# The weights' lower parts made by VectorE alone, in a two-layer decoder trunk on one core

## The chip, the cores and the metric

The kernel runs on one core of a Trainium2 chip, as one program. The metric is the device time of one execution in microseconds, the median of the runs shown. Before the change it is 2773.92 us (three runs: 2771.38, 2773.92 and 2775.31).

## The reference, cut to what matters

Two layers, each of four sub-layers, in float32 on 512 tokens of width 1024. Every sub-layer stands between two RMS norms, and its output is added to the residual `x`:

```
for l in range(2):
    h = rmsnorm(x, ff1_pre_g[l])
    x = x + 0.5 * rmsnorm(swiglu(h, ff1_w1[l], ff1_w3[l], ff1_w2[l]), ff1_post_g[l])
    h = rmsnorm(x, mix_pre_g[l])
    x = x + rmsnorm(token_mixer(h, ...), mix_post_g[l])        # pooling, sparse attention, gated MLP
    h = rmsnorm(x, mem_pre_g[l])
    x = x + rmsnorm(memory_cross_attention(h, ...), mem_post_g[l])
    h = rmsnorm(x, ff2_pre_g[l])
    x = x + 0.5 * rmsnorm(swiglu(h, ff2_w1[l], ff2_w3[l], ff2_w2[l]), ff2_post_g[l])
```

Nearly all the arithmetic is products of the 512 tokens with weight matrices that are read once each; the queue that brings them moves 255.56 MB.

## The kernel before, in words

**Products in parts.** A float32 operand is cut into an upper part (rounded to the matmul type fp32r) and a lower part (what the rounding left). A product is then three matmuls: upper by upper, upper by lower, lower by upper (`mm3`). So each weight block of 128x1024 numbers passes through four hands: a DMA from SP's queue brings it into one of three buffers `raw`; ScalarE copies it, rounded, into the upper half of one of four buffers `wh` (L394); then one subtraction, raw minus upper, fills the lower half; then TensorE uses both. The subtraction is the instruction that the change is about. `Weights.parts` issues it through `Builder.lo`, which adds up two estimates, one for VectorE (a start when its modelled queue is free, 0.07 us and 1.05 ns per column) and one for GpSimd (0.1 us and 2.4 ns per column). GpSimd gets it if its estimated end is earlier than VectorE's plus `self.spare`.

**`spare`** is the allowance, in us, that the program sets by stage: -0.5 at first; 4.0 from the last loop of `token_out` to the middle of the next `first_blocks`; 2.5 in the mixer, from the second compression to the end of `spatial`. With two idle queues and 1024 columns GpSimd's estimate is 2.56 us and VectorE's 1.15 us, so it is GpSimd at 4.0 and at 2.5, and VectorE at -0.5.

**Order.** The order of all engines' instructions is written out by the host before the run. `Clock` is a model of the engines: tasks are generators in a heap, each resumed at its modelled time, and what a task issues stands in its engine's queue in that order. Each engine runs its queue in order. Every modelled end therefore moves what comes after it in all the queues, TensorE's among them. The model has one free time per engine, and no case in which two engines hold each other up.

**Boundaries.** Each sub-layer ends in `token_out`: four tiles of 128 tokens (m = 0 to 3), each with two banks of 512 columns, and the last four weight blocks of the second half are used tile by tile, so that the tiles end one after another. A tile that is done goes through `chain`: sum of squares (ScalarE), product with the gain (VectorE, `f<-ps,f`), the sum `sty<-ssy`, one small step, the power on GpSimd (`sty<-v,neghalf`, L468), the update of the residual in two halves on VectorE (`x<-f,sty,x`, L402, both inputs in SBUF), squares of the new `x` on ScalarE, a second power on GpSimd (`st`), the pre-norm of the next sub-layer on VectorE (`f<-x,st,f`, L402), eight transposes on TensorE (L437), and the split into `hh` (ScalarE) and `hlo` (VectorE). `first_blocks` starts the next sub-layer: four weight blocks by the first 256 tokens as soon as tiles 0 and 1 are split, then the same four blocks by the last 256 tokens when tiles 2 and 3 are. There are seven such boundaries between the eight sub-layers. The four `wh` buffers are held by the last four blocks of `token_out` until its last tile, so the four blocks of `first_blocks` are made in the boundary itself.

Of the kernel before, what the change touches and what calls it, by code (L numbers as in the profile page):

```python
# [10 lines left out]
F32 = mybir.dt.float32  # L11
# [3 lines left out]
OP = mybir.AluOpType  # L15
# [152 lines left out]
class Slots:  # L168


    def __init__(self, tiles):
        self.free = [(0.0, i, t) for i, t in enumerate(tiles)]
        self.n = len(self.free)
        self.gone = ()
# [133 lines left out]
class Weights:  # L308
# [39 lines left out]
    def parts(self, k):  # L348
        b, n = self.b, k.cols
        raw, hi, lo = k.raw[:, :n], k.hl[:, 0, :n], k.hl[:, 1, :n]  # L350
        yield b.act(hi, raw, AF.Copy)
        r = b.lo(lo, raw, hi)
        self.raws.put(r, k.raw)
        k.raw = None
        k.ready = r
        self.pump()
# [21 lines left out]
def size(ap):  # L378
    n = 1
    for s in ap.shape[1:]:  # L380
        n *= s
    return n


class Builder:
    def __init__(self, tc, d, out):
        self.tc, self.nc, self.d, self.out = tc, tc.nc, d, out
        self.ck = Clock()
        self.spare = -0.5

# [19 lines left out]
    def gtt(self, out, a, b, op):  # L412
        self.nc.gpsimd.tensor_tensor(out, a, b, op)  # L413
        return self.ck.op("g", 0.1 + 0.0024 * size(out))

    def lo(self, out, src, hi):

        ck = self.ck
        n = size(out)
        v = max(ck.free["v"], ck.now) + 0.07 + 0.00105 * n  # L420
        g = max(ck.free["g"], ck.now) + 0.1 + 0.0024 * n
        if g < v + self.spare:
            return self.gtt(out, src, hi.bitcast(F32), OP.subtract)
        return self.tt(out, src, hi.bitcast(F32), OP.subtract)

    def mm(self, out, w, x, first, last):
        ck = self.ck
# [19 lines left out]
    def split(self, hi, lo, src, scale=None, bias=None):  # L447

        if scale is not None:
            yield self.act(hi, src, AF.Copy, scale=scale)  # L450
            return self.stt(lo, src, scale, hi.bitcast(F32), OP.mult, OP.subtract)
        if bias is not None:
            yield self.act(hi, src, AF.Identity, bias=bias)
            return self.stt(lo, src, bias, hi.bitcast(F32), OP.add, OP.subtract)
        yield self.act(hi, src, AF.Copy)
        return self.tt(lo, src, hi.bitcast(F32), OP.subtract)
# [134 lines left out]
    def first_blocks(self, keys):  # L591

        ck = self.ck
        got = []
        for m in (0, 1):
            ck.reach(("T", self.at, m))
        for key in keys:
            blk, bank = self.ws.next(key), ck.get(self.ps)
            self.proj(blk, bank, 0, 256)
            got.append((blk, bank))  # L600
        for m in (2, 3):
            ck.reach(("T", self.at, m))
        self.spare = -0.5
        for blk, bank in got:
            self.proj(blk, bank, 256, 512)
            self.ws.release(blk)
            yield bank

    def token_out(self, l, ph, name, lhs, ready, nk, scale, tail):

        nc, ck, ws = self.nc, self.ck, self.ws
        a, b = scale
        pg = self.load_gain(l, ph, "post")
        after = self.after
        norm = self.pre_norms(self.at + 1, self.load_gain(*after, "pre")) if after else None
        ws.ahead = 4
        nb = nk // 2
        tail = min(tail, nb)
        t0 = {}
        left = [2 * NT]  # L620

        def products(blk, i, m, bank):
            for kk in range(2):
                k = 2 * i + kk
                c = slice(kk * 512, (kk + 1) * 512)
                lh, ll = lhs(k, m)
                self.mm(bank, lh, blk.hl[:, 0, c], k == 0, False)
                self.mm(bank, lh, blk.hl[:, 1, c], False, False)
                self.mm(bank, ll, blk.hl[:, 0, c], False, k == nk - 1)

        def squares(m, h, bank):
            t = yield from ck.take(self.f)
            r = self.act(self.junk, bank, AF.Square, accum_out=self.ssy[:, m, h:h + 1])
            q = self.tt(t[:, :512], bank, pg[h][:, :512], OP.mult)
            left[0] -= 1
            if not left[0]:
                self.f.put(q, *pg)
            self.ps.put(max(r, q), bank)
            return t, r, q

        def half(m, bank):
            t, r, q = yield from squares(m, 0, bank)
            t0[m] = (t, max(r, q))

        def chain(m, bank):
            t1, r, q = yield from squares(m, 1, bank)
            yield r
            st = self.small.tile([128, 2], F32, name="sty", bufs=6)
            yield self.tt(st[:, 0:1], self.ssy[:, m, 0:1], self.ssy[:, m, 1:2], OP.add)
            yield (yield from self.rstd(st[:, 1:2], st[:, 0:1], a, b))  # L650
            xs = [self.x[:, m, h * 512:(h + 1) * 512] for h in range(2)]
            rs = []
            for h, t in enumerate((t0[m][0], t1)):
                r = self.stt(xs[h], t[:, :512], st[:, 1:2], xs[h], OP.mult, OP.add)
                self.f.put(r, t)
                rs.append(r)
            for h in range(2):
                yield rs[h]
                if after:
                    r = self.act(self.junk, xs[h], AF.Square, accum_out=self.ssx[:, m, h:h + 1])  # L660
                else:
                    nc.sync.dma_start(self.out[m * 128:(m + 1) * 128, h * 512:(h + 1) * 512], xs[h])
            if after:
                yield r
                yield from norm(m)

        banks = [ck.get(self.ps) for _ in range(NT)]
        for i in range(nb):
            for kk in range(2):
                ck.reach(ready(2 * i + kk))  # L670
            blk = ws.next((l,) + name + (0, i))
            for m in range(NT):
                products(blk, i, m, banks[m])
            ws.release(blk)
        for m in range(NT):
            ck.spawn(half(m, banks[m]), ck.now + ck.LAT)
        banks = [ck.get(self.ps) for _ in range(NT)]
        for i in range(nb - tail):
            blk = ws.next((l,) + name + (1, i))
            for m in range(NT):  # L680
                products(blk, i, m, banks[m])
            ws.release(blk)
        blks = []
        self.spare = 4.0
        for m in range(NT):
            for i in range(tail):
                if m == 1:
                    ws.ahead = 2
                if m == 0:
                    blks.append(ws.next((l,) + name + (1, nb - tail + i)))  # L690
                blk = blks[i]
                products(blk, nb - tail + i, m, banks[m])
                if m == NT - 1:
                    ws.release(blk)
            ck.spawn(chain(m, banks[m]), ck.now + ck.LAT + (2.0 if m == 2 and after else 0.0))
# [44 lines left out]
    def mixer(self, l, ph):  # L740
        tc, nc, d, ck = self.tc, self.nc, self.d, self.ck
        F, H, PS, ws, at = self.f, self.hl, self.ps, self.ws, self.at
        with tc.tile_pool(name=f"mix{l}", bufs=1) as pool, \
# [152 lines left out]
            def compress(s, i):  # L896
                if i == 0:
                    ck.reach(("B", at, s))
                    hid[s] = (ck.get(PS), ck.get(PS))
                blk = ws.next((l, "cw1", s, i))  # L900
                for a in range(4):
                    lp = 4 * i + a
                    mv = B[s][lp // 8][:, (lp % 8) * 64:(lp % 8) * 64 + 64]
                    for hh in range(2):
                        self.mm(hid[s][hh][:, :64], blk.raw[:, a * 256 + hh * 128:a * 256 + hh * 128 + 128], mv,
                                lp == 0, lp == 15)
                ws.release(blk)
# [95 lines left out]
                        self.mm(o, self.hlo[:, k, t], blk.hl[:, 0, c], False, k == KD - 1)  # L1003
                ws.release(blk)

            self.spare = 2.5
            compress(1, 0)
            vb = [ck.get(PS) for _ in range(NT)]
            for i in range(4):
# [121 lines left out]
            def spatial():  # L1131
                ck.reach(("wst", at))
                for m in range(NT):
                    ck.reach(("vg", at, m))
                for g in range(4):
                    bank = ck.get(PS)
                    for m in range(NT):
                        self.mm(bank[:, m * 128:(m + 1) * 128], VG[m][:, g * 128:(g + 1) * 128],
                                wst[:, g * 128:(g + 1) * 128], True, True)
                    ck.spawn(gate_units(g, bank), ck.now + ck.LAT)  # L1140
                F.put(ck.now, *VG, wst, rows["lng"], rows["lnb"], rows["gm"])
                self.spare = -0.5

            tasks = self.attention(few, dict(KS=KS, KW=KW, V=V, VC=VC, Q=Q, gates=gates, msel=msel, mwin=mwin,
                                                 mcmp=mcmp, zero=zero, rows=rows))
# [432 lines left out]
```

## Time and profile before

| | us |
|---|---|
| median of the runs shown | 2773.92 |
| the profiled execution | 2770.11 |
| its span, first to last instruction | 2768.1 |
| TensorE busy in matmuls | 2716.3 |
| VectorE busy | 1420.6 |
| ScalarE busy | 1037.9 |
| GpSimd busy | 323.8 |

The profiled execution lies 3.8 us under the median of the runs and 2.0 us over its span. Its mean granted TensorE clock is 0.997 of full speed. In the 40 slices of the span TensorE is at nine tenths or more in 38. The chain that ended last is 88% TensorE and 9% VectorE.

Names in the rows: PE is TensorE, PEld its weight load, DVE is VectorE, ACT ScalarE, POOL GpSimd, SP the DMA queue. L429 is a matmul, L437 a transpose, L394 any ScalarE activation, L398 any `tensor_tensor` and L402 any `scalar_tensor_tensor` of VectorE, L413 any `tensor_tensor` of GpSimd: one line serves many places, so the tiles' names tell which one it is. `wh<-raw,wh` is always the subtraction that makes a lower part.

### The profile page before, as it was taken

What the parts mean: (1) busy time and instruction counts of PE and PEld (TensorE: products, weight loads), DVE (VectorE), ACT (ScalarE), POOL (GpSimd) and SP (SyncE); (2) the same over time, 40 slices, a digit from 0 to 9 for tenths busy, and PEclk for the clock granted to TensorE, in tenths of its full rate; (3) what the DMA queues carried; (4) which work ended last, traced back from release to release, by engine and by line L of the source; (5) the groups of instructions that cost most, each with busy time, mean ns of one, the idle gap of its engine ahead of it and who ended that gap; (6) DMA issues with size and microseconds to landing.
All of it is one profiled execution on the core that took longest, in us unless ns stands there. A gap on an engine that the chain in (4) does not pass through costs nothing.

```text
span 2768.1 us, 34462 instructions
## 1 busy us (share of the span) xinstructions
PE 2716.3 (98%) x13624; PEld 2298.3 (83%) x13624; DVE 1420.6 (51%) x2536; ACT 1037.9 (37%) x1894; POOL 323.8 (12%) x299
## 2 busy tenths in 40 slices
PE   7999999999999999999999999999999999999998
PEld 7888888887888888888888888888778898888887
DVE  4443254889536564432354432639885465544422
ACT  3222234456435443222232222435564354432222
POOL 0000021411222020000010000213112220200000
PEclk9999999999999999999999999999999999999999
DMA  3232223311233322322223322242122343223222
GB/s 145 96 114 96 99 92 123 101 58 62 84 114 122 115 77 99 114 99 98 78 99 106 108 93 98 89 135 88 54 69 80 111 138 107 73 103 107 99 92 76
DMA packets 77971, 270.45 MB, mean 98 GB/s; under 512 B 10161, under 2 KB 10673, under 8 KB 77809
## 3 DMA queue, kind: packets, MB, share of 16 engines
q1 hardware_dynamic: 71568, 255.56, 27.3%
q0 software_dynamic: 3136, 10.25, 1.5%
q10 hardware_dynamic: 3104, 2.45, 0.3%
q8 instruction: 106, 1.74, 0.3%
q14 instruction: 57, 0.46, 0.1%
HBM read 266.12 MB, written 2.10 MB: 97 GB/s over the span
## 4 chain that ended last, share of the span: by engine, by line
PE 88%; DVE 9%; ACT 1%; issue 1%; POOL 1%; DMA 0%; ACTq 0%; SPq 0%; DVEq 0%; POOLq 0%
PE ps L429 85%; PE ps L437 2%; DVE x L402 2%; DVE hl L398 1%; ACT junk L394 1%; DVE wh L398 1%; DVE f L402 1%; DVE f L407 1%; DVE f L398 1%; DVE ast L398 1%; DVE f L1227 1%; DVE mf L407 0%; DVE mf L1227 0%; DVE sty L398 0%; DMA raw<-in_ff_w_dram 0%
## 5 line engine op out<-in xcount | busy, mean ns | idle before, releaser
L429 PE MATMUL ps<-hh,wh 128*128 128x512 f32 (+1 forms) x4864 | 1399.1, 369 | 1.9 <-ACT hh L394 1.4
L429 PEld LDWEIGHTS ps<-hh,wh 128*128 128x128 f32 x4864 | 883.9, 189 | 149.9 <-ACT hh L394 1.8
L429 PE MATMUL ps<-hlo,wh 128*128 128x512 f32 (+1 forms) x2432 | 897.3, 369 | 0.1
L398 DVE TENSOR_TENSOR wh<-raw,wh 128x1024 fp32r<-128x1024 f32 x402 | 505.6, 1260 | 601.8 <-ACT wh L394 601.2
L394 ACT ACTIVATE wh<-raw 128x1024 fp32r<-128x1024 f32 x462 | 485.2, 1052 | 726.3 <-PE ps L429 430.5
L429 PEld LDWEIGHTS ps<-hlo,wh 128*128 128x128 f32 x2432 | 460.8, 189 | 72.4 <-DVE v L409 0.4
L429 PE MATMUL ps<-wh,hl 128*128 128x512 f32 x2016 | 468.9, 390 | 0.0
L429 PEld LDWEIGHTS ps<-wh,hl 128*128 128x128 f32 x2016 | 376.8, 188 | 77.2
L413 POOL TENSOR_TENSOR wh<-raw,wh 128x1024 fp32r<-128x1024 f32 (+2 forms) x60 | 146.7, 2449 | 1281.9 <-ACT wh L394 1281.9
L398 DVE TENSOR_TENSOR f<-ps,f 128x512 f32<-128x512 f32 (+1 forms) x169 | 116.6, 690 | 313.9 <-PE ps L429 209.5
L429 PE MATMUL ps<-wh,g 128*128 128x512 f32 x960 | 222.2, 390 | 0.0
L429 PEld LDWEIGHTS ps<-wh,g 128*128 128x128 f32 x960 | 179.3, 188 | 36.7
L429 PE MATMUL ps<-hl,wh 128*128 128x512 f32 (+1 forms) x960 | 194.9, 350 | 0.0
L429 PEld LDWEIGHTS ps<-hl,wh 128*128 128x128 f32 x960 | 152.3, 190 | 20.5
L394 ACT ACTIVATE hl<-f 128x512 fp32r<-128x512 f32 (+1 forms) x75 | 47.3, 630 | 252.6 <-DVE f L398 213.0
L437 PE MATMUL ps<-ident,f 128*128 128x128 f32 (+1 forms) x573 | 100.7, 285 | 33.2 <-DVE f L402 30.9
L394 ACT ACTIVATE hl<-ps 128x512 fp32r<-128x512 f32 (+2 forms) x180 | 80.4, 468 | 102.4 <-PE ps L429 81.7
L398 DVE TENSOR_TENSOR hl<-ps,hl 128x512 fp32r<-128x512 f32 (+2 forms) x180 | 91.8, 528 | 43.5 <-ACT hl L394 42.1
L437 PEld LDWEIGHTS ps<-ident,f 128*128 128x128 f32 (+1 forms) x573 | 70.4, 143 | 48.6 <-DVE f L402 36.3
L402 DVE SCALAR_TENSOR_TENSOR f<-f,ps 128x512 f32<-128x512 f32 x120 | 81.7, 681 | 46.4 <-PE ps L429 42.0
L394 ACT ACTIVATE g<-f 128x512 fp32r<-128x512 f32 x40 | 25.3, 632 | 181.2 <-DVE f L398 181.2
L402 DVE SCALAR_TENSOR_TENSOR x<-f,sty,x 128x512 f32<-128x512 f32 x64 | 78.5, 1267 | 10.2 <-POOL sty L468 10.2
(186 smaller groups left out, 1991.7 us busy)
## 6 DMA issues: line engine op xcount, KB each, us to landing
raw<-in_ff_w_dram SPq DMA_DIRECT2D x264, 512.0 KB, 3.5
raw<-in_wf_dram SPq DMA_DIRECT2D x80, 512.0 KB, 3.5
raw<-in_cw_dram SPq DMA_DIRECT2D x16, 512.0 KB, 3.6
raw<-in_wmo_dram SPq DMA_DIRECT2D x16, 512.0 KB, 3.5
raw<-in_wq_dram SPq DMA_DIRECT2D x16, 512.0 KB, 3.6
raw<-in_wk_dram SPq DMA_DIRECT2D x16, 512.0 KB, 3.8
raw<-in_wv_dram SPq DMA_DIRECT2D x16, 512.0 KB, 3.8
raw<-in_wo_dram SPq DMA_DIRECT2D x16, 512.0 KB, 3.6
```

The costliest lines, as they stand in the source:

```text
L394: self.nc.scalar.activation(out, src, func, accum_out=accum_out, **kw)
L398: self.nc.vector.tensor_tensor(out, a, b, op)
L402: self.nc.vector.scalar_tensor_tensor(out, a, s, b, op0, op1)
L407: self.nc.vector.tensor_scalar(out, a, s0, None, op0=op0)
L413: self.nc.gpsimd.tensor_tensor(out, a, b, op)
L429: self.nc.tensor.matmul(out, w, x, start=first, stop=last)
L437: self.nc.tensor.transpose(out, src, self.ident)
L1227: nc.vector.tensor_tensor_reduce(p[:, po:po + w], bank[:, ps:ps + w], mask, -0.125, 3.0e38, OP.add, OP.min, st[:, br, 0:1])
```

## The change

The choice is taken out: `Builder.lo` and the five places that set `spare` go, and `Weights.parts` always issues the subtraction on VectorE, with the same operands. The estimate that the planner books for it is VectorE's.

```diff
@@ class Weights, parts
         yield b.act(hi, raw, AF.Copy)
-        r = b.lo(lo, raw, hi)
+        r = b.tt(lo, raw, hi.bitcast(F32), OP.subtract)
         self.raws.put(r, k.raw)
@@ class Builder
-        self.spare = -0.5
...
-    def lo(self, out, src, hi):
-
-        ck = self.ck
-        n = size(out)
-        v = max(ck.free["v"], ck.now) + 0.07 + 0.00105 * n
-        g = max(ck.free["g"], ck.now) + 0.1 + 0.0024 * n
-        if g < v + self.spare:
-            return self.gtt(out, src, hi.bitcast(F32), OP.subtract)
-        return self.tt(out, src, hi.bitcast(F32), OP.subtract)
@@ first_blocks
-        self.spare = -0.5
@@ token_out
-        self.spare = 4.0
@@ mixer
-            self.spare = 2.5
...
-                self.spare = -0.5
```

GpSimd keeps its other work: the powers of the norms, the element-wise products and sums of the mixer (`gtt` elsewhere), copies of zeros, and the DMAs of gains and biases.

## Rows read from the trace of the kernel before

**Rows 1.** The page, busy us (share of the span) xinstructions by engine.
```profile
PE 2716.3 (98%) x13624; PEld 2298.3 (83%) x13624; DVE 1420.6 (51%) x2536; ACT 1037.9 (37%) x1894; POOL 323.8 (12%) x299
```
**Rows 2.** Waits of TensorE over the span: total us, times, longest us.
```profile
PE ps L437 <- DVE f L402: 30.9, 18, 8.0
```
**Rows 3.** GpSimd's subtractions: xcount: ns min/median/max, first and last start us, forms.
```profile
L413 POOL TENSOR_TENSOR wh<-raw,wh x60: 1401/2405/3187, 362.5 to 2740.3; 128x1024 fp32r<-128x1024 f32 x54, 128x840 fp32r<-128x840 f32 x4, 128x560 fp32r<-128x560 f32 x2
```
**Rows 4.** Windows over the seven boundaries (28 us each): their sum and mean.
```profile
sum 196.00, PE 178.65 PEld 164.10 DVE 156.10 ACT 96.30 POOL 99.08; mean PE 25.52 PEld 23.44 DVE 22.30 ACT 13.76 POOL 14.15
```
**Rows 5.** Timeline of GpSimd in one boundary: start us, us, instruction.
```profile
1384.59 2.41 POOL L413 TENSOR_TENSOR wh<-raw,wh 128x1024 fp32r<-128x1024 f32 x1 [1.59 <-ACT wh L394]
...
1387.87 5.21 POOL L413 TENSOR_TENSOR wh<-raw,wh 128x1024 fp32r<-128x1024 f32 x2
...
1395.67 2.51 POOL L413 TENSOR_TENSOR wh<-raw,wh 128x1024 fp32r<-128x1024 f32 x1
```
**Rows 6.** Timeline of VectorE in the same boundary.
```profile
1385.73 1.29 DVE L398 TENSOR_TENSOR sty<-ssy 128x1 f32<-128x1 f32 x1
...
1388.32 5.31 DVE L402 SCALAR_TENSOR_TENSOR x<-f,sty,x 128x512 f32<-128x512 f32 x2
...
1395.21 3.52 DVE L402 SCALAR_TENSOR_TENSOR x<-f,sty,x 128x512 f32<-128x512 f32 x2 [0.39 <-POOL sty L468]
1398.65 1.40 DVE L402 SCALAR_TENSOR_TENSOR f<-x,st,f 128x512 f32<-128x512 f32 x2
...
1406.14 0.69 DVE L398 TENSOR_TENSOR hlo<-ps,hh 128x512 fp32r<-128x512 f32 x1 [0.70 <-ACT hh L394]
```
**Rows 7.** Timeline of TensorE there: first block, late transposes, second halves.
```profile
1388.28 0.28 PE L429 MATMUL ps<-hh,wh 128*128 128x256 f32 x1
...
1399.45 1.12 PE L437 MATMUL ps<-ident,f 128*128 128x128 f32 x4 [2.74 <-DVE f L402]
...
1404.88 0.60 PE L437 MATMUL ps<-ident,f 128*128 128x128 f32 x4
1405.23 0.48 PE L429 MATMUL ps<-hh,wh 128*128 128x256 f32 x2
```
**Rows 8.** Windows there: PE, PEld, DVE, ACT, POOL busy (x), PEclk, DMA share, GB/s.
```profile
1388.00:1396.00 8.00, 8.00 (x67) 7.92 (x67) 7.54 (x10) 4.03 (x8) 6.45 (x5) 1.00 0.55 196
1400.00:1403.00 3.00, 3.00 (x18) 3.00 (x17) 2.05 (x6) 1.20 (x2) 0.55 (x1) 0.62 0.24 94
```
**Rows 9.** Window there of VectorE alone: DVE busy (x), PEclk, DMA share, GB/s.
```profile
1383.00:1407.00 24.00, 20.07 (x26) 0.93 0.25 88
```
**Rows 10.** VectorE by tile over the span: xcount: ns min/median/max, first and last start.
```profile
L402 DVE SCALAR_TENSOR_TENSOR x<-f,sty,x x64: 739/750/2889, 369.2 to 2764.0; 128x512 f32<-128x512 f32 x64
L398 DVE TENSOR_TENSOR sty<-ssy x32: 142/149/1760, 368.1 to 2762.3; 128x1 f32<-128x1 f32 x32
...
L398 DVE TENSOR_TENSOR wh<-raw,wh x402: 1204/1225/2674, 14.0 to 2734.8; 128x1024 fp32r<-128x1024 f32 x134
```
**Rows 11.** VectorE by shape over the span: xcount | busy us, mean ns | idle before.
```profile
L402 DVE SCALAR_TENSOR_TENSOR x<-f,sty,x 128x512 f32<-128x512 f32 x64 | 78.5, 1267 | 10.2 <-POOL sty L468 10.2
...
L398 DVE TENSOR_TENSOR sty<-ssy 128x1 f32<-128x1 f32 x32 | 15.9, 498 | 0.0
```
**Rows 12.** GpSimd's powers by tile: xcount: ns min/median/max, first and last start.
```profile
L468 POOL TENSOR_TENSOR sty<-v,neghalf x32: 547/548/560, 368.6 to 2762.8; 128x1 f32<-128x1 f32 x32
L468 POOL TENSOR_TENSOR brs<-v,neghalf x8: 544/656/997, 505.0 to 1884.2; 128x1 f32<-128x1 f32 x8
```
**Rows 13.** Windows of the mixers' stretch with 2.5, both layers (columns as rows 8).
```profile
462.00:524.00 62.00, 61.14 (x350) 53.40 (x349) 33.95 (x55) 22.18 (x47) 29.15 (x15) 1.00 0.41 133
1836.00:1898.00 62.00, 60.01 (x349) 52.53 (x349) 37.32 (x56) 22.44 (x48) 28.60 (x15) 1.00 0.40 125
```
**Rows 14.** VectorE in the first of these: one shape by groups, as rows 11.
```profile
L398 DVE TENSOR_TENSOR V<-f,V 128x256 fp32r<-128x256 f32 x3 | 3.5, 1153 | 0.0
```
**Rows 15.** Timeline of VectorE there: one of these three.
```profile
521.12 0.42 DVE L398 TENSOR_TENSOR V<-f,V 128x256 fp32r<-128x256 f32 x1
```

## The prediction, made before the changed kernel was run

> **What bounds the kernel now.** The page's busy times come first: the reader is to see that TensorE is busy 2716.3 of 2768.1 us, so that only 52 us of the span are without a matmul, and that VectorE, which is to take work over, is busy 51% [rows 1]. On the average it has room; what counts is where TensorE waits. The second view is the list of TensorE's waits: its one large entry is the transposes that wait for VectorE's `f`, 30.9 us in 18 waits [rows 2]. The longest, 8.0 us, is the program's first, which waits for the first tile's norm; most of the rest falls into the boundaries between sub-layers. So the third view is a table of windows over the seven boundaries: 196.00 less 178.65, or 17.35 us, of idle TensorE, 2.5 us each [rows 4]. The fourth is the timeline of one boundary engine by engine, to see who is late there.
>
> The one at 1383 to 1407 us (cross-attention to the second FFN of layer 0) reads so. TensorE starts the four first blocks at 1388.28 [rows 7]. It issues 67 matmuls in 8.00 us, 0.12 us each [rows 8], so the first halves of four blocks (4 x 24 matmuls) take 11.5 us, and the 16 transposes of tiles 2 and 3, at 0.60 us per four [rows 7], 2.4 us. Without a wait the second halves would start at 1402.2; they start at 1405.23. The 3.0 us between are the 2.74 us for which the transposes wait for `f<-x,st,f`, and a slower stretch behind it: the granted clock is 0.62 at 1400 to 1403, where it was 1.00 before TensorE stood still [rows 8].
>
> Why is `f` late? VectorE is at it from 1383 on, busy 20.07 of 24 us [rows 9], but much of that isn't work. The two halves of `x<-f,sty,x` take 5.31 us and later 3.52 us as pairs [rows 6], while one has a median of 0.75 us and a largest of 2.89 [rows 10]. The long ones end when GpSimd's subtractions end: 1387.87 + 5.21 = 1393.08 against 1388.32 + 5.31 = 1393.63, and 1395.67 + 2.51 = 1398.18 against 1395.21 + 3.52 = 1398.73 [rows 5, 6], a last clean half behind each. Even the sum of two columns, `sty`, takes 1.29 us beside the first subtraction, against 0.15 alone [rows 5, 6, 10]. GpSimd's subtraction holds up VectorE's instructions with two SBUF inputs, and these are links of the norm chain.
>
> **The change part by part.** 60 subtractions leave GpSimd, some 144 us of its time at the median of 2.4 us [rows 3]. By `spare` they are five at each of seven boundaries, one before the last tiles of the program, and twelve in each mixer: 35 + 1 + 24 = 60.
>
> *VectorE gets the boundaries' subtractions.* Of the five, the first is for the last block of `token_out`, made well ahead; four stand in the chain's time. One costs VectorE 1.225 us (median of 402) [rows 10], four 4.9 us, over seven boundaries 34.3 us.
>
> *VectorE loses the holds.* Over the span `x<-f,sty,x` has a mean of 1.267 us over 64 and `sty` one of 0.498 over 32 [rows 11], against medians of 0.750 and 0.149 [rows 10]: 64 x 0.517 + 32 x 0.349 = 33.1 + 11.2 = 44.3 us, all of it where GpSimd subtracts. In the boundary above it is 5.31 + 3.52 less four clean halves of 0.75, and 1.29 less 0.15: 5.8 + 1.1 = 6.9 us.
>
> *Sum for the boundaries.* VectorE's time to the last `hlo` (1406.83 above [rows 6]) shrinks by 44.3 - 34.3 = 10.0 us over seven boundaries if its idle time there stays. That is the lower end. The upper end is TensorE's 3.0 us of each boundary, 21 us, reached if the subtractions fall into VectorE's idle 3.9 us [rows 9], in which it waits for ScalarE and for the powers. Placing them by hand in the boundary above: the chain's next steps and subtractions 1 and 2 up to the first `x` pair at 1389.7, that pair to 1391.1, the third tile's product with its small sums to 1392.3, subtraction 3 to 1393.5, the second `x` pair to 1394.9, subtraction 4 to 1396.1, then `f`. Its first half is done at 1396.9, not 1399.4, and TensorE comes to these transposes at 1396.7 (2.74 us before 1399.45 [rows 7]). The wait all but goes, and the stretch of slow clock with it. What is late next is the last tile's split, for which VectorE still has a few us of work. I take the middle, 15 us.
>
> *The powers.* GpSimd's power is a link of the chain, twice per tile. It reads SBUF too, and now it can meet a subtraction on VectorE. `sty`'s powers took 0.547 to 0.560 us in all 32 cases; those of the mixer's `brs`, beside two-input instructions of VectorE, 0.544 to 0.997 [rows 12]. So a meeting costs 0 to 0.45 us, and four powers per boundary 0 to 12.6 us in all. In the placing above they run while VectorE does `f<-ps,f`, `hlo` or nothing, and in a boundary GpSimd has now nothing else before them in its queue; nearest are the 32 even ones, and I take 0. The Trainium skill (SBUF — State Buffer, "SBUF: two separate sides") states the hold as a rule: the shared ports are an exclusive lock, and whichever of a two-input VectorE instruction and a GpSimd instruction that reads SBUF starts first has it for its whole length. The trace agrees for VectorE's side (2.89 us against 0.75). The rule speaks against the change in one place: it would let a power wait for a whole subtraction, and with 1.225 us for each of 28 powers the sum would be 34 us slower instead of 12.6 at most; no row shows such a power.
>
> *The mixers.* In the stretches with 2.5 TensorE is idle 0.86 and 1.99 us of 62 [rows 13]; there is little to win. VectorE is busy 33.95 and 37.32 us there and gets eleven subtractions, at most 13.5 us at 1.225 us each, for which it has room. It loses holds of the same kind: three `V<-f,V` take 3.5 us, where a free one takes 0.42 [rows 14, 15], so 2.2 us by these alone. But the subtractions now stand in one queue with the gated values' work. The bounds are -2.9 us (all idle gone) and +6 (each mixer's blocks late by 3 us, about what TensorE loses where it waits for VectorE at a boundary); I take 0.
>
> *What hangs on it.* SP's loads: a `raw` buffer is free at the subtraction's end, 1.2 us behind the upper part and not 2.4, so the next load leaves earlier unless the subtraction waits in VectorE's queue. Up to 362.5 us, GpSimd's first subtraction [rows 3], nothing changes. Behind that the planner books other ends, so the order in all queues shifts a little; for the attention stages this is a change without a sign, some us either way. The subtraction before the end of the program is off its chain: 0.
>
> Total: -15 us, from the profiled execution's 2770.1 to 2755; on the median, 3.8 us higher, 2759.
>
> **The rivals.** *Half of it comes* (chance 0.18): the wait at the second tile's transposes goes, but TensorE then stands at the last tile, whose split follows VectorE's whole queue. For it: 4.9 us more work between. Against: 3.9 us idle to take it up. Gain 2 to 9 us: 2765 to 2772.
>
> *The mixers give it back* (0.09): VectorE's queue there delays the blocks' lower parts by more than their lead, up to two blocks. Against it: TensorE hardly waits there now. The result is within 5 us of 2774.
>
> *Slower: subtractions at the head of VectorE's queue* (0.16). VectorE runs in order. A subtraction that the planner puts before a link of the chain, and whose upper part ScalarE delivers late, stops the chain while VectorE idles; on GpSimd such a wait cost nothing. ScalarE's queue is in order as well, and the third and fourth blocks' upper parts stand there behind the squares of the residual. If that adds 2.5 to 3.5 us of idle VectorE to each boundary, against 1.4 us (10.0 / 7) saved, the seven cost 8 to 15 us: 2782 to 2789. It decides from 1.4 us of such idle time per boundary on. For it: GpSimd's own gap before the first of the four is 1.59 us [rows 5]. Against: that gap was spent before the buffers came free. The Trainium skill (Perfetto Trace Analysis, "Optimizing Scalar/DVE Operations") gives the general case for this side, that with a saturated VectorE some work may be offloaded even to GpSimd, and the doubt in the same place, that between these two it might not help because they share a read port. This trace bears out the doubt: 44.3 us of holds against 34.3 us of work moved.
>
> **How the numbers follow.** The forecast, 10 to 23 us faster, has 0.53; more than that through a luckier order 0.04. With the three rivals it makes 1. A measurement of this kernel tells 0.2%, 5.5 us, from no change. Faster by more is the forecast, the lucky order and half of the first rival: 0.66. Within it are that rival's other half and the second: 0.18. Slower: 0.16. The range is 2747 (21 us and the mixers' 2.9 off, with the runs' spread of some 3 us) to 2777, which holds all but the slower rival and the luckiest order; the likeliest case alone gives 2751 to 2764.
>
> **What would show it.** In the trace after, `x<-f,sty,x` and `sty` have their medians as means; no L413 writes `wh`; GpSimd is busy some 180 us; VectorE's total rises by about 72 us of subtractions less the holds, to about 1430 us. The seven windows' idle time falls from 17.35 us to under 6, and no slow clock follows it. The forecast is wrong if that idle time stays, or shows up at `hlo` or at `wh`, or if VectorE waits for ScalarE's `wh` in the boundaries; powers longer than 0.6 us would say that the new hold is the dearer one.

## The result, and the profile after

The changed kernel takes 2753.56 us (median of five runs, 2752.76 to 2753.91), the kernel before 2773.92 (2771.19 to 2775.31). The ratio is 0.9929, with a 95% interval of 0.9915 to 0.9942: 20.4 us faster by the medians, 16 to 24 by the interval, where 15 were forecast. The profiled execution took 2753.62 us, its span is 2751.8. Line numbers have moved: L398, L402, L429, L437 and L468 of before are L397, L401, L418, L426 and L457. The kernels of the experiments have line numbers of their own; the tiles' names tell which instruction a row shows.

The busy times of the page after answer to [rows 1]:

```profile
PE 2712.1 (99%) x13624; PEld 2293.9 (83%) x13624; DVE 1412.2 (51%) x2596; ACT 1038.2 (38%) x1894; POOL 191.4 (7%) x239
```

VectorE has 60 instructions more and is busy 8.4 us less. TensorE is busy 4.2 us less with the same 13624 matmuls, and idle 12.1 us less: together the 16.3 us by which the span is shorter than the 2768.1 us of before. The waits of TensorE in the kernel after (columns as [rows 2]):

```profile
PE ps L426 <- DVE f L401: 17.6, 15, 7.3
PE ps L418 <- DVE wh L397: 5.7, 4, 1.4
PE ps L426 <- DVE hl L397: 4.1, 4, 1.8
```

The wait for `f` has fallen from 30.9 to 17.6 us. Of both, some 12.3 us lie in the program's first 22 us, so what is left at the boundaries has fallen from 18.5 to 5.3 us. The four waits for `hl`, in the attention stages, were there before too (4.1 us). A new one has come: four waits of up to 1.4 us for a lower part, each some 7 us ahead of one of the windows that follow. The sum of windows over the same seven boundaries (at 370, 838, 1005, 1369, 1735, 2202 and 2369 us, 28 us each), against [rows 4]:

```profile
sum 196.00, PE 190.72 PEld 171.63 DVE 155.26 ACT 105.59 POOL 39.69; mean PE 27.25 PEld 24.52 DVE 22.18 ACT 15.09 POOL 5.67
```

TensorE's idle time there is 5.28 us and was 17.35 (19.0 if the windows before are begun 3 us earlier, as these are by the first blocks). The clock has changed with it. Three of the seven windows before had a mean granted clock of 0.94 and the other four 1.00; after, all seven have 1.00. One of the three, in the kernel before, and the same boundary after (columns as [rows 8]):

```profile
1378.00:1406.00 28.00, 25.26 (x166) 23.32 (x165) 22.17 (x32) 13.47 (x27) 13.33 (x10) 0.94 0.21 76
```
```profile
1369.00:1397.00 28.00, 27.66 (x186) 24.91 (x185) 22.37 (x43) 14.98 (x32) 5.29 (x7) 1.00 0.22 75
```

Three windows of 28 us at 0.94 are 5 us of full speed lost (an estimate), which is about what TensorE's busy time has lost. Over the span the mean granted clock is 0.995 to 0.998 in every run of the kernel before for which it is on record, and 0.999 or 1.000 in every run of the changed kernel. The times of the kernel before go with it: 2768.9 to 2770.9 us at 0.998, 2777.2 at 0.995. So a part of the gain is that TensorE keeps its full clock; and the profiled execution of before, at 0.997, is one of the faster ones, 16.5 us over that of the changed kernel where the medians are 20.4 apart.

Now the boundary of [rows 5 to 9], which lies 5.4 us earlier. It is the one between the second FFN of layer 0 and the first FFN of layer 1, the fourth of the seven; the one from the cross-attention to the second FFN of layer 0, as which the prediction names it, is the third, at 1005 us. GpSimd:

```profile
1382.47 1.40 POOL L457 TENSOR_TENSOR sty<-v,neghalf 128x1 f32<-128x1 f32 x1 [4.76 <-DVE v L408]
1387.38 0.55 POOL L457 TENSOR_TENSOR sty<-v,neghalf 128x1 f32<-128x1 f32 x1 [3.52 <-DVE st L397]
1387.90 1.19 POOL L457 TENSOR_TENSOR st<-v,neghalf 128x1 f32<-128x1 f32 x1
```

VectorE:

```profile
1380.38 1.22 DVE L397 TENSOR_TENSOR wh<-raw,wh 128x1024 fp32r<-128x1024 f32 x1
...
1382.24 1.22 DVE L397 TENSOR_TENSOR wh<-raw,wh 128x1024 fp32r<-128x1024 f32 x1
...
1383.97 1.40 DVE L401 SCALAR_TENSOR_TENSOR x<-f,sty,x 128x512 f32<-128x512 f32 x2
...
1385.96 1.22 DVE L397 TENSOR_TENSOR wh<-raw,wh 128x1024 fp32r<-128x1024 f32 x1
...
1387.45 1.23 DVE L397 TENSOR_TENSOR wh<-raw,wh 128x1024 fp32r<-128x1024 f32 x1
1388.60 1.41 DVE L401 SCALAR_TENSOR_TENSOR x<-f,sty,x 128x512 f32<-128x512 f32 x2
1389.92 1.41 DVE L401 SCALAR_TENSOR_TENSOR f<-x,st,f 128x512 f32<-128x512 f32 x2
```

TensorE:

```profile
1382.92 0.28 PE L418 MATMUL ps<-hh,wh 128*128 128x256 f32 x1
...
1390.72 0.66 PE L426 MATMUL ps<-ident,f 128*128 128x128 f32 x4
...
1395.30 0.60 PE L426 MATMUL ps<-ident,f 128*128 128x128 f32 x4
1395.66 0.36 PE L418 MATMUL ps<-hlo,wh 128*128 128x256 f32 x1
```

The pairs of `x<-f,sty,x` take 1.40 and 1.41 us instead of 5.31 and 3.52, with four subtractions between the chain's links. Two of GpSimd's three powers are long: both met a subtraction of VectorE and end 0.41 us behind its end (1383.46 and 1388.68). `f` starts 7.0 us behind the first block's first matmul and not 10.4; its transposes have no wait. From that first matmul to the second halves it is 12.7 us; before it was 16.95 [rows 7]. The granted clock of this stretch in the kernel after, against 0.62 in [rows 8]:

```profile
1390.00:1393.00 3.00, 3.00 (x27) 2.83 (x26) 2.51 (x7) 1.68 (x6) 0.55 (x1) 1.00 0.54 178
```

VectorE by tile over the span, against [rows 10]:

```profile
L401 DVE SCALAR_TENSOR_TENSOR x<-f,sty,x x64: 739/744/753, 369.6 to 2747.8; 128x512 f32<-128x512 f32 x64
L397 DVE TENSOR_TENSOR sty<-ssy x32: 144/149/154, 368.6 to 2746.1; 128x1 f32<-128x1 f32 x32
...
L397 DVE TENSOR_TENSOR wh<-raw,wh x462: 733/1225/2676, 14.0 to 2724.0; 128x1024 fp32r<-128x1024 f32 x152, 128x560 fp32r<-128x560 f32 x2
```

Not one of the 64 is long. The subtractions still reach 2.68 us, in the mixers. GpSimd's powers by tile, against [rows 12]:

```profile
L457 POOL TENSOR_TENSOR st<-v,neghalf x32: 543/548/1440, 5.4 to 2391.0; 128x1 f32<-128x1 f32 x32
L457 POOL TENSOR_TENSOR sty<-v,neghalf x32: 547/554/1460, 369.0 to 2746.5; 128x1 f32<-128x1 f32 x32
L457 POOL TENSOR_TENSOR brs<-v,neghalf x8: 548/988/1469, 504.4 to 1872.3; 128x1 f32<-128x1 f32 x8
```

The hold has turned round: a power on one column now takes up to 1.47 us where a subtraction runs on VectorE. Last, the mixers' stretches, against [rows 13]:

```profile
462.00:524.00 62.00, 62.00 (x362) 54.45 (x361) 35.71 (x67) 22.72 (x48) 3.99 (x4) 1.00 0.39 129
1820.00:1882.00 62.00, 62.00 (x355) 54.12 (x354) 36.86 (x68) 22.77 (x49) 3.99 (x4) 1.00 0.41 134
```

TensorE stands still no more there, and with eleven and twelve subtractions more VectorE is busy 1.8 us longer in the first and 0.5 us less in the second.

### The profile page after: what moved, and what is told of

Its sections match the earlier page's. It is cut to its first block, busy times and chain, and to the rows that moved or that the text cites. A ratio compares the mean times of both kernels' runs of the same rounds, so it can differ in the third digit from the quotient of the medians.

```text
span 2751.8 us, 34461 instructions
## 1 busy us (share of the span) xinstructions
PE 2712.1 (99%) x13624; PEld 2293.9 (83%) x13624; DVE 1412.2 (51%) x2596; ACT 1038.2 (38%) x1894; POOL 191.4 (7%) x239
## 4 chain that ended last, share of the span: by engine, by line
PE 91%; DVE 5%; ACT 2%; issue 1%; DMA 0%; POOL 0%; ACTq 0%; SPq 0%; DVEq 0%; POOLq 0%
PE ps L418 89%; PE ps L426 2%; ACT junk L393 1%; DVE wh L397 1%; DVE hl L397 1%; DVE f L401 0%; DVE x L401 0%; ACT wh L393 0%; DMA raw<-in_ff_w_dram 0%; DVE f L406 0%; DVE f L397 0%; DVE f L1212 0%; DVE ast L397 0%; DVE mf L406 0%; DVE mf L1212 0%
## 5 line engine op out<-in xcount | busy, mean ns | idle before, releaser
L418 PE MATMUL ps<-hh,wh 128*128 128x512 f32 (+1 forms) x4864 | 1393.9, 368 | 1.4 <-ACT hh L393 1.4
L418 PEld LDWEIGHTS ps<-hh,wh 128*128 128x128 f32 x4864 | 880.8, 189 | 148.7 <-ACT hh L393 1.8
L397 DVE TENSOR_TENSOR wh<-raw,wh 128x1024 fp32r<-128x1024 f32 x462 | 577.0, 1251 | 644.2 <-ACT wh L393 643.4
L418 PE MATMUL ps<-hlo,wh 128*128 128x512 f32 (+1 forms) x2432 | 897.0, 369 | 0.1
L418 PEld LDWEIGHTS ps<-hlo,wh 128*128 128x128 f32 x2432 | 459.1, 189 | 72.8 <-DVE v L408 0.4
L418 PE MATMUL ps<-wh,hl 128*128 128x512 f32 x2016 | 469.7, 390 | 2.9 <-DVE wh L397 2.9
L418 PEld LDWEIGHTS ps<-wh,hl 128*128 128x128 f32 x2016 | 376.5, 188 | 81.0 <-DVE wh L397 3.7
L397 DVE TENSOR_TENSOR f<-ps,f 128x512 f32<-128x512 f32 (+1 forms) x169 | 116.7, 690 | 300.1 <-PE ps L418 214.6
L418 PE MATMUL ps<-wh,g 128*128 128x512 f32 x960 | 222.2, 390 | 0.0
L418 PEld LDWEIGHTS ps<-wh,g 128*128 128x128 f32 x960 | 179.3, 188 | 36.8
L418 PE MATMUL ps<-hl,wh 128*128 128x512 f32 (+1 forms) x960 | 194.5, 350 | 0.0
L418 PEld LDWEIGHTS ps<-hl,wh 128*128 128x128 f32 x960 | 152.3, 190 | 20.5
L426 PE MATMUL ps<-ident,f 128*128 128x128 f32 (+1 forms) x573 | 98.9, 282 | 19.9 <-DVE f L401 17.6
L397 DVE TENSOR_TENSOR hl<-ps,hl 128x512 fp32r<-128x512 f32 (+2 forms) x180 | 92.0, 528 | 44.3 <-ACT hl L393 41.9
L457 POOL TENSOR_TENSOR sty<-v,neghalf 128x1 f32<-128x1 f32 x32 | 23.5, 734 | 1219.1 <-DVE v L408 1201.6
L401 DVE SCALAR_TENSOR_TENSOR f<-f,ps 128x512 f32<-128x512 f32 x120 | 81.7, 681 | 44.0 <-PE ps L418 39.6
L426 PEld LDWEIGHTS ps<-ident,f 128*128 128x128 f32 (+1 forms) x573 | 69.7, 141 | 35.0 <-DVE f L401 22.9
L397 DVE TENSOR_TENSOR hl<-f,hl 128x512 fp32r<-128x512 f32 (+1 forms) x75 | 54.0, 720 | 49.9 <-ACT hl L393 49.7
```

What stands on the lines that cost most here:

```text
L397: self.nc.vector.tensor_tensor(out, a, b, op)
L401: self.nc.vector.scalar_tensor_tensor(out, a, s, b, op0, op1)
L418: self.nc.tensor.matmul(out, w, x, start=first, stop=last)
L426: self.nc.tensor.transpose(out, src, self.ident)
L457: self.nc.gpsimd.tensor_tensor(out, v[:, :n], self.neghalf[:, :n], OP.pow)
```

## The experiments

Theory: GpSimd's subtraction holds up VectorE's instructions, and these are on the norm chain (*hold*). Rivals: the planner's other order (*order*); lower parts that are ready earlier (*latency*); GpSimd's queue, in which the powers stand behind subtractions (*queue*). Each time is beside runs of the kernel before on the same chip.

**1. The old order, executed by VectorE.** From the kernel before:

```diff
         if g < v + self.spare:
-            return self.gtt(out, src, hi.bitcast(F32), OP.subtract)
+            self.nc.vector.tensor_tensor(out, src, hi.bitcast(F32), OP.subtract)
+            return ck.op("g", 0.1 + 0.0024 * n)
```

> The planner books every subtraction as the kernel before did (GpSimd's estimate where it chose GpSimd), so the order in all queues stays that of before; but VectorE executes all of them. Theory hold (GpSimd's subtraction locks VectorE's two-input instructions out): most of the 20.4 us comes, 2755 to 2762 us, and x<-f,sty,x has 0.75 us as its mean. Theory order (the gain is the new order): stays at 2770 to 2778 us. Theory latency (the lower parts are ready 1.2 us earlier): like hold in time, so this run does not part these two.

2752.4 us, ratio 0.9926 (0.9913 to 0.9938), below the range expected: all of the gain without the new order.

**2. The new order, executed by GpSimd.** From the kernel before:

```diff
         if g < v + self.spare:
-            return self.gtt(out, src, hi.bitcast(F32), OP.subtract)
+            self.nc.gpsimd.tensor_tensor(out, src, hi.bitcast(F32), OP.subtract)
+            return ck.op("v", 0.07 + 0.00105 * n)
```

> The other way round: where the old rule picks GpSimd (by the new bookings), GpSimd executes the subtraction, but the planner books VectorE's estimate, which is close to the order of after. Theory hold: back at 2768 to 2782 us, x<-f,sty,x up to 2.9 us again. Theory order: 2752 to 2758 us.

2774.96 us, ratio 1.0009 (1.0000 to 1.0018): none of the gain. Its order is near that of the changed kernel. With run 1 this settles *order*: the engine makes the difference. VectorE's updates by tile in run 2, and TensorE's waits:

```profile
L402 DVE SCALAR_TENSOR_TENSOR x<-f,sty,x x64: 741/751/2901, 369.7 to 2768.9; 128x512 f32<-128x512 f32 x64
```
```profile
PE ps L438 <- DVE f L402: 34.4, 18, 7.5
...
PE ps L430 <- POOL wh L423: 2.1, 2, 1.9
```

The 2.9 us are back, and with them the wait for `f`. The second row speaks on *latency*: even when GpSimd makes the lower parts, TensorE waits for them 2.1 us in all, and in the kernel before it was less:

```profile
PE ps L429 <- POOL wh L413: 0.4, 1, 0.4
```

So at most 0.4 us of the gain can be TensorE's waits for GpSimd's lower parts. (That loads leave earlier because a raw buffer comes free earlier is not tested by itself.)

**3. The boundaries alone.** From the kernel before, the mixers as they were:

```diff
-        self.spare = 4.0
+        self.spare = -100.0
```

> Only the boundaries' subtractions (35 and the last one) go to VectorE; the mixers keep their allowance of 2.5 and GpSimd. Theory hold at the boundaries, as predicted: 2757 to 2761 us (13 to 17 us of the 20.4), TensorE's idle time in the seven boundaries under 6 us. Rival, that the mixers gave the gain: 2768 us or more.

2757.84 us against 2771.92, ratio 0.9946 (0.9934 to 0.9959): 14 us by the medians, 11 to 18 by the interval. TensorE's idle time in the seven boundaries is 5.4 us (windows as those of the result), as in the changed kernel.

**4. The mixers alone.** From the kernel before:

```diff
-            self.spare = 2.5
+            self.spare = -100.0
```

> Only the mixers' 24 subtractions go to VectorE; the boundaries keep 4.0 and GpSimd. By the trace after, the mixers' stretches lose some 5 us less of TensorE than before: 2767 to 2771 us. Forecast as it stood (mixers at 0): 2773 to 2775 us. Rival, that the mixers gave most: under 2762 us.

2769.57 us, ratio 0.9988 (0.9979 to 0.9997): 1 to 6 us faster. On top of the boundaries the mixers bring 4 to 5 us (2757.84 to 2753.6 and 2752.8 for the changed kernel). So about 70% of the gain comes from the boundaries.

**5. Hold against queue: a second subtraction that reads.** From the kernel after; `more` is on where `spare` was 4.0:

```diff
         r = b.tt(lo, raw, hi.bitcast(F32), OP.subtract)
+        if b.more:
+            b.nc.gpsimd.tensor_tensor(raw, raw, hi.bitcast(F32), OP.subtract)
```

> The kernel after, but at the boundaries GpSimd does each subtraction a second time, once VectorE has made the lower part, into the raw buffer that is then dead (a wasted 2.4 us of GpSimd with two SBUF inputs, not booked by the planner). The lower parts are as early as after. Theory hold: the boundaries' gain goes, 2766 to 2785 us, x<-f,sty,x up to 2.9 us. Theory latency: stays within 3 us of the run with writes only.

**6. Its control, which only writes.**

```diff
+        if b.more:
+            for _ in range(3):
+                b.nc.gpsimd.memset(raw, 0.0)
```

> The control for the run before: in the same places GpSimd fills the dead raw buffer three times with zeros (some 2.7 us, an estimate from its small fills), which reads nothing. GpSimd's queue is as long and the raw buffer as late. Theory hold: x<-f,sty,x stays at 0.75 us, and the time stays near after but for powers that queue behind the fills, 2754 to 2766 us. If the lost time was GpSimd's queue and not the hold, this run is as slow as the one with reads.

Run 5 takes 2827.11 us (ratio 1.0194), run 6 2805.75 (1.0116), both beyond what was expected of them. The mistake was GpSimd's queue: a wasted instruction that starts behind VectorE's subtraction stands before the next power. Groups of VectorE's updates, with the idle time before them, in run 5:

```profile
L404 DVE SCALAR_TENSOR_TENSOR x<-f,sty,x 128x512 f32<-128x512 f32 x64 | 59.8, 976 | 27.7 <-POOL sty L460 27.7
```

and in run 6:

```profile
L405 DVE SCALAR_TENSOR_TENSOR x<-f,sty,x 128x512 f32<-128x512 f32 x64 | 45.2, 748 | 50.6 <-POOL sty L461 50.6
```

GpSimd's wasted instructions in the two runs, and the pages' busy times:

```profile
L354 POOL TENSOR_TENSOR raw<-raw,wh 128x1024 f32<-128x1024 f32 x36 | 86.8, 2412 | 1151.4 <-DVE wh L400 1099.6 <-DVE v L411 23.3 <-ACT wh L396 20.3
PE 2730.3 (97%) x13624; PEld 2310.6 (82%) x13624; DVE 1454.7 (52%) x2596; ACT 1038.5 (37%) x1894; POOL 275.0 (10%) x275
```
```profile
L355 POOL MEMSET raw<- 128x1024 f32 x108 | 102.5, 953 | 1146.9 <-DVE wh L401 1091.2 <-DVE v L412 23.2 <-ACT wh L397 20.3
PE 2727.9 (97%) x13624; PEld 2309.1 (82%) x13624; DVE 1413.2 (50%) x2596; ACT 1038.1 (37%) x1894; POOL 283.4 (10%) x347
```

With fills the updates keep their 0.748 us, though GpSimd is busy about as long (three fills for one subtraction), and VectorE's busy time is that of the changed kernel within 1 us; with reads the updates' mean is 0.976, and VectorE is busy 42.5 us more with the same instructions. What holds VectorE in these runs is that GpSimd reads SBUF. The 52 us of run 6 over the changed kernel are the price of a power that waits in the queue and of a raw buffer that comes free later, which this pair doesn't part; the 21 us from run 6 to run 5 go with the hold, at a queue nearly as long. In the kernel before the queue matters little: a power started over 2 us late, behind a subtraction, at two boundaries only, and elsewhere within 0.4 us. Those two, from the first FFN to the mixer, are the ones that gained least: TensorE's idle time in their windows went from 2.59 and 2.33 us to 1.79 and 1.87, in each of the other five from over 2 to at most 0.4.

**7. GpSimd's products on VectorE too.** From the kernel after, in `gtt`:

```diff
-        self.nc.gpsimd.tensor_tensor(out, a, b, op)
-        return self.ck.op("g", 0.1 + 0.0024 * size(out))
+        return self.tt(out, a, b, op)
```

> The kernel after, with all of the mixers' element-wise products and sums of GpSimd (some 60 of 512 columns) on VectorE too. They still hold VectorE up: some of its subtractions take 2.0 to 2.7 us. If the hold is the dearer part there as well: 2 to 6 us less, 2748 to 2752. If VectorE is the bound in the attention stage (95% busy there): 2756 to 2765, slower than after.

2743.21 us, ratio 0.9892 (0.9879 to 0.9906): some 10 us better than the change, and better than either range expected. Windows of the attention stages (600 us and the like of layer 1) in the kernel after:

```profile
600.00:660.00 60.00, 56.91 (x294) 45.12 (x293) 57.77 (x203) 39.99 (x116) 14.35 (x26) 1.00 0.16 54
1975.00:2035.00 60.00, 55.31 (x285) 43.82 (x284) 56.07 (x174) 36.80 (x96) 15.73 (x22) 1.00 0.21 71
```

and in run 7:

```profile
600.00:660.00 60.00, 59.87 (x304) 48.26 (x302) 56.64 (x187) 37.87 (x101) 2.51 (x15) 1.00 0.22 71
1970.00:2030.00 60.00, 59.88 (x300) 48.38 (x299) 54.62 (x177) 36.35 (x94) 2.27 (x12) 1.00 0.23 71
```

TensorE's idle 3.1 and 4.7 us go to 0.1 each. What VectorE does in these windows can't be compared, as they hold other shares of the work (203 and 187 instructions in the first). Over the span, by the page, with the largest group of the added products:

```profile
PE 2710.3 (99%) x13624; PEld 2295.8 (84%) x13624; DVE 1422.7 (52%) x2656; ACT 1037.6 (38%) x1894; POOL 96.0 (4%) x179
L397 DVE TENSOR_TENSOR f<-f,f 128x512 f32<-128x512 f32 x22 | 15.2, 690 | 0.6
```

VectorE has 60 instructions more than in the changed kernel. At 0.69 us each they are 41 us of work, but its busy time rises by 10.5 us only: some 31 us of holds went. No subtraction is long any more:

```profile
L397 DVE TENSOR_TENSOR wh<-raw,wh x462: 737/1226/1459, 14.2 to 2715.2; 128x1024 fp32r<-128x1024 f32 x152, 128x560 fp32r<-128x560 f32 x2
```

**8. Only the merged branches' sums.**

```diff
-                yield self.gtt(mv, mv, tv, OP.add)
+                yield self.tt(mv, mv, tv, OP.add)
```

> The kernel after, with only the sums of the merged branches moved to VectorE; the pooling windows and the gated products stay on GpSimd. These sums hold seven to nine subtractions of VectorE up by about 1 us each. Hold: 2750 to 2753. If TensorE has slack there, no change: 2753 to 2755.

2752.53 us, ratio 0.9926 (0.9914 to 0.9939): not told from the change. TensorE's waits for `hl` in the attention stages are the same 4.1 us here and are not in run 7's list. So taking these sums' holds away gave nothing that can be measured, and run 7's gain goes with the gated products and the pooling windows; those two were not run apart.

**9. Run 7 with run 1's bookings.** The two edits above, together.

> All subtractions and all of the mixers' products on VectorE, but the subtractions booked with GpSimd's estimates as in the run that kept the old order, in which the powers of sty were held for 0.1 us in sum and not 5.9. The two gains should add: 2740 to 2743 us. If the held powers lay beside other waits: 2743 to 2745.

2742.91 us: not told from run 7, and at the limit between the two ranges expected. The longest power of `sty` is 0.574 us here, so these powers were not what the end waited for.

**10. Run 7 with the boundaries' subtractions in halves.**

```diff
-        r = b.tt(lo, raw, hi.bitcast(F32), OP.subtract)
+        if b.more:
+            for s in (slice(0, n // 2), slice(n // 2, n)):
+                r = b.tt(lo[:, s], raw[:, s], hi[:, s].bitcast(F32), OP.subtract)
+                if s.start == 0:
+                    yield r
+        else:
+            r = b.tt(lo, raw, hi.bitcast(F32), OP.subtract)
```

> All products on VectorE, and each subtraction of a boundary cut into two of 512 columns, the second issued a planner's step later, so that a power can slip in between. If the new hold of the powers costs time: the powers' excess over 0.55 us falls from some 10 to under 5 us in sum, and the time to 2738 to 2742 us. If it doesn't: 2743 to 2746, as two halves take about 0.1 us more than one whole.

2749.71 us: a miss, 6.5 us slower than run 7. TensorE's waits in run 10 tell where:

```profile
PE ps L432 <- DVE f L408: 22.7, 18, 6.9
PE ps L424 <- DVE wh L404: 3.6, 4, 0.9
```

The wait for `f` is 22.7 us, 17.9 in run 7. The halves take 0.682 us each, 0.14 more than one whole, and change the order; which of the two it was stays open. Nor did the edit do what it was for: the longest power of `st` is still 1.527 us, and all of them together are 8.1 us over 0.548 us each, where run 7 has 10.0. So what shorter powers would be worth is not shown by this run.

**11. The changed kernel beside runs 9 and 10.**

> The changed kernel itself, on the same chip as the two others, so that they are compared with it directly: 2752 to 2755 us.

2752.84 us, ratio 0.9922 (0.9908 to 0.9935).

**12. Four subtractions back to GpSimd.** One of the four new waits for `wh` in the changed kernel (VectorE, then TensorE):

```profile
994.27 2.85 DVE L397 TENSOR_TENSOR f<-ps,f 128x512 f32<-128x512 f32 x4 [4.79 <-ACT junk L393]
997.03 1.21 DVE L397 TENSOR_TENSOR wh<-raw,wh 128x1024 fp32r<-128x1024 f32 x1
```
```profile
998.30 0.73 PE L418 MATMUL ps<-wh,mh 128*128 128x512 f32 x2 [1.43 <-DVE wh L397]
```

The last block's subtraction stands behind the gain products of four tiles. From run 7:

```diff
+                k.last = key[1] in ("wmo", "wo") and key[-2:] == (1, 3)
...
-        r = b.tt(lo, raw, hi.bitcast(F32), OP.subtract)
+        if k.last:
+            b.nc.gpsimd.tensor_tensor(lo, raw, hi.bitcast(F32), OP.subtract)
+            r = b.ck.op("g", 0.1 + 0.0024 * n)
+        else:
+            r = b.tt(lo, raw, hi.bitcast(F32), OP.subtract)
```

> The kernel with the mixers' products on VectorE (2743.2 us), but four subtractions go back to GpSimd: those of the very last weight block of the mixer's and the cross-attention's output product, which on VectorE stand behind four gain products, and for which TensorE waits 1.43 us at four places in the changed kernel. The gain products read PSUM and one SBUF tile, so nothing should be held there. If this new wait is the price of the moved fifth subtraction: 2735 to 2739 us, and TensorE's 5.7 us of waits for wh gone. If it lies beside another wait: 2742 to 2745.

2736.32 us, ratio 0.9862 (0.9846 to 0.9879), the best of all: 38 us under the kernel before. All of TensorE's waits in run 12 that are listed:

```profile
PE ps L430 <- DVE f L406: 17.9, 15, 7.5
PE ps L422 <- ACT hh L398: 1.4, 1, 1.4
```

The four waits are gone, and the time with them (6.9 us under run 7 by the medians, for 5.7 us of waits).

## Why the prediction was right

*The mechanism* was the predicted one. Runs 1 and 2 put the whole gain on the executing engine, runs 5 and 6 tie the hold to GpSimd's reading, and no update in the rows after is longer than 0.753 us.

*The boundaries*, 15 us between 10 and 21: 14 (run 3). That the two lie so close is in part luck, as the working holds less well than its sum. One term was too large: 0.60 us for four transposes. [Rows 7] themselves show the next matmul 0.35 us behind their start; with that the second halves could have started at 1388.3 + 11.5 + 1.4 = 1401.2, and 4.0 us were lost in that boundary, not 3.0. After, all of it is back (12.7 us where 12.9 were to be had). Nor was this boundary like the others: in the profiled execution a slow clock came behind three of the seven only, and two gained 0.8 and 0.5 us of idle time. Against the gain stands the next point, which the sum didn't have.

*The fifth subtraction* was called "made well ahead" and cost nothing. That holds for the boundary that was worked by hand, behind an FFN. It was wrong at four of the seven: behind the mixer and the cross-attention the output product has only four blocks in each half, and VectorE does the first half's four gain products just then. TensorE waits 5.7 us, one of the prediction's own signs of being wrong (idle time that shows up at `wh`), and run 12 shows the price to be real. That is part of the slower rival, a subtraction placed badly in VectorE's queue, in a smaller form: it stood behind the chain's work instead of stopping it. The rival as it was put, VectorE idle at the head of its queue, appears at the two boundaries from the first FFN to the mixer: in the first of them VectorE idles 0.19 and 0.60 us before subtractions, for ScalarE's `wh`. TensorE still waits 1.8 and 1.9 us for `f` there; how much of that is due to it is not shown.

*The powers* were taken at 0 with 0.45 us as the far end of one meeting. A meeting costs up to 0.9 us, to just behind the subtraction's end, and in the boundary that was worked by hand two met, where the placing had none. So the rule that the Trainium skill gives (SBUF — State Buffer, "SBUF: two separate sides") was the better guide to the size: the trace after agrees, 1.46 us beside a subtraction against 0.55 alone. The 34 us that the prediction worked out by it were far off: by the groups of the powers of `sty` and `st` the sum is 23.5 + 21.2 us, where it was 17.6 + 17.5. And run 9, without `sty`'s share, is no faster than run 7. The prediction's sign that powers over 0.6 us would make the new hold the dearer one misled: they are 9.6 us longer in sum, where VectorE lost some 80 us of holds.

*The mixers* were taken at 0 and bring 4 to 5 us on top of the boundaries, beyond the end of -2.9 (alone, in run 4, 1 to 6). TensorE's idle time of 0.86 and 1.99 us went to zero, as far as that end reached; the rest was not worked out, for the holds there were not added up. Over the span VectorE's busy time was forecast to come to about 1430 us, 72 us of subtractions less 62 of holds; it is 1412.2, so the holds were some 80 us. The order that the planner made, left without a sign, is worth nothing that can be measured (run 1 against the change).

*The doubt about a saturated VectorE* that the Trainium skill names (Perfetto Trace Analysis, "Optimizing Scalar/DVE Operations") came out on the side of its second half: the change moved some 72 us of subtractions to VectorE, and VectorE's busy time fell by 8.4 us. In run 7 it rose, by 10.5 us for 41 us of products, and the kernel was faster still.

## What to carry to other kernels

An instruction that takes several times its median beside another engine's work is a wait that no list of waits shows; compare largest and median by tile before believing that an engine is full. Moving work between two engines that hold each other up is to be priced by the holds it removes, which may exceed the work, and by whether the engine that sets the time waits behind them: run 8 took holds away and gained nothing. When work joins a queue, look at what stands there at that moment for every one of the moved instructions: four of sixty cost as much as a third of the gain.

## What the runs showed of the hardware that was not expected

An instruction of VectorE with a single SBUF tile as input is held too. In the kernel before, GpSimd and then VectorE:

```profile
514.14 5.25 POOL L413 TENSOR_TENSOR wh<-raw,wh 128x1024 fp32r<-128x1024 f32 x2 [0.95 <-ACT wh L394]
```
```profile
517.06 2.36 DVE L409 TENSOR_SCALAR gates<-gates 128x24 f32<-128x24 f32 x1
...
521.45 0.17 DVE L409 TENSOR_SCALAR gates<-gates 128x24 f32<-128x24 f32 x1
```

Twenty-four columns take 2.36 us and end as GpSimd's second subtraction ends (519.39), where the next one alone takes 0.17. And a power on a single column is held for 0.9 us by VectorE's subtraction, while three fills of 1024 columns on GpSimd left VectorE's updates at 0.748 us.
